# A first token tile projected without its norm factor, and re-split later on GpSimd: the opening stage of a hybrid encoder block

## The chip, the cores and the metric

The kernel runs on one core of a Trainium2 chip. The time is device microseconds of one execution of the whole program, taken as the median of the runs. Names used below: PE is TensorE (matrix products, and transposes as products with an identity), DVE is VectorE, ACT is ScalarE, POOL is GpSimd, SP is SyncE, which issues most of the DMAs. "PEclk" is the share of TensorE's full clock that the chip granted.

## The reference

One layer of an encoder on 512 tokens of width 2048, all in float32. What matters here is its very beginning:

```
def rmsnorm(x, w):
    x32 = x.astype(F32)
    y = x32 * lax.rsqrt(jnp.mean(x32 * x32, axis=-1, keepdims=True) + EPS) * w.astype(F32)
...
        h = rmsnorm(x, norm_w[layer])
        proj = h @ w_in[layer]
        (a_q, a_f, a_i, a_g, c_q, c_kv, k_idx_raw, w_idx_raw, b_g, m_a, m_b) = jnp.split(
            proj, SPLIT_POINTS, axis=-1)
```

Each token has one norm factor, 1 / sqrt(mean of its squares + EPS). Behind the projection come a gated linear recurrence (branch A), an attention over selected keys (branch B), gates, an output projection, the residual and a last norm. Since the factor is one number for each token, h @ W is the factor times (x * w) @ W, token by token.

## The kernel before, in words

Every float32 product is made of three: each operand is split into a high half, which is the value rounded to the product's own number format, and a low half, the rest; high x high, low x high and high x low are added in PSUM. A split costs one copy (the high half, on ScalarE) and one subtraction (the low half, on VectorE or GpSimd).

The program is a list of jobs that are written out one after the other; each engine runs its instructions in the order in which they are written. There is no scheduler: the order in the text is the order on the engine, and engines wait for each other by semaphores alone. The first job that works is `start`. It normalises x, transposes it to [channel, token], splits it into the tiles `xh` and `xl`, which all later projections read, and meanwhile projects 272 columns (256 of `a_i` for the first pair of heads, 16 of the index weights) so that TensorE has something to do. It does so by 4 token tiles t of 128 tokens, and for each of these by 4 groups g of 4 x 128 channels:

- `turn(t, g)` (L313): four transposes of x on TensorE into a PSUM bank `pt`.
- `square(t, i)` (L299): ScalarE squares half a tile of x and sums it along the row. `rstd(t)` (L302, L303) adds the two sums on VectorE and takes the root on ScalarE; `on_diag(t)` (L306, L307) takes the reciprocal and writes it on the diagonal of a 128x128 matrix; `spread()` (L339, L341) multiplies this with ones on TensorE, which gives the factor as a row over tokens in all partitions, and copies it out of PSUM.
- For t = 0: `weigh` (L318) multiplies the transposed x with the norm weight, and the `scaled` at L399 multiplies the result with the factor once this is known. For t = 1 to 3, `follow(t)` does both in one instruction for each 128 channels (L350).
- `high(t, g)` (L322, ScalarE) writes the high half into `xh`, `low(t, g)` (L326) the low half into `xl`: on VectorE, and for t > 0 and odd g on GpSimd.
- The weights come in four blocks `fr` of 512 rows x 272 columns. `w_high(i)` (L330, ScalarE) and `w_low(i)` (L333) split them into `fh` and `fl`; the last block's low half is made on GpSimd.
- `project(t)` makes the products of tile t, 4 groups of 12 (L81: for each group four high x high, four low x high, four with the low weights), and in the middle, ahead of group 2, writes out `follow(t + 1)`. At the end the result is copied to `hv` (L384, ScalarE) and `widx` (L385, VectorE).

Ahead of the last two groups of tile 3 `prep(0)` splits the first weights of the next job (L72 on ScalarE, L73 on VectorE); that job (`kx`, L76 to L78) starts on TensorE as soon as the last product of `project(3)` is through. Of the other names: `ident` is an identity matrix, `wc` holds the norm weight by channel, `st` the sums and factors, `rrow` the factor's row. The loads are issued by SyncE (L272 for x, L277 for the weights); a load may be issued only when the one eight places ahead has landed.

Of the kernel before, what the change touches and what calls it, by code (L numbers as in the profile page):

```python
# [26 lines left out]
F32 = mybir.dt.float32  # L27
# [7 lines left out]
T, D = 512, 2048  # L35
# [15 lines left out]
def hybrid_block(ctx, tc, x, norm_w, w_in, lb_table, gnorm_a, q_norm_w, kv_norm_w, w_uq,  # L51
# [198 lines left out]
    def start():  # L250
# [8 lines left out]
        ys = [p0.tile([128, 4, 128], F32, name=f"y{g}") for g in range(4)]  # L259
        diag = p0.tile([128, 128], F32, name="diag")  # L260
        sq = p0.tile([128, HF], mybir.dt.bfloat16, name="sq")
# [8 lines left out]
        def load_x(t):  # L270
            for i in range(2):
                SP.dma_start(xs[t][i], x2[t * 128:(t + 1) * 128, i * HF:(i + 1) * HF])  # L272

        def load_w(i):
# [16 lines left out]
        for _ in range(4):  # L291
            PE.matmul(warm[:, 0:128], ones, ones, start=True, stop=True)
# [3 lines left out]
        V.tensor_copy(wc, pw[:, 0:16])  # L296

# [19 lines left out]
        def weigh(pt, g):  # L317
            V.tensor_tensor(ys[g], pt.rearrange("p (j t) -> p j t", j=4),  # L318
                            wc[:, g * 4:g * 4 + 4, None].to_broadcast([128, 4, 128]), op=OP.mult)

        def high(t, g):
            A.activation(xh[g][:, :, t * 128:t * 128 + 128], ys[g], AF.Copy)  # L322

        def low(t, g):
            o = slice(t * 128, t * 128 + 128)
            (G if t and g % 2 else V).tensor_tensor(xl[g][:, :, o], ys[g], xh[g][:, :, o].bitcast(F32),  # L326
                                                    op=OP.subtract)

        def w_high(i):
            A.activation(wh[i], raw[i], AF.Copy)  # L330
# [6 lines left out]
        def spread():  # L337
            pr = mmp.tile([128, T], F32, name="acc")
            PE.matmul(pr[:, 0:128], ones, diag, start=True, stop=True)  # L339
            r = p0.tile([128, 128], F32, name="rrow", bufs=2)  # L340
            V.tensor_copy(r, pr[:, 0:128])  # L341
            return r

        def follow(t):
            pts = [turn(t, g) for g in range(4)]
            r = spread()

            def scaled(g):
                for j in range(4):
                    V.scalar_tensor_tensor(ys[g][:, j, :], pts[g][:, j * 128:j * 128 + 128],  # L350
                                           wc[:, g * 4 + j:g * 4 + j + 1], r, op0=OP.mult, op1=OP.mult)
                high(t, g)

            scaled(0)
            scaled(1)
            low(t, 0)
            if t < 3:
                square(t + 1, 0)
            scaled(2)
            low(t, 1)  # L360
            if t < 3:
                square(t + 1, 1)
            scaled(3)
            if t < 3:
                rstd(t + 1)
            low(t, 2)
            if t < 3:
                on_diag(t + 1)
            low(t, 3)

        def project(t):
            o = slice(t * 128, t * 128 + 128)
            acc = mmp.tile([128, T], F32, name="acc")
            for g in range(4):
                if g == 2:
                    if t < 3:
                        follow(t + 1)
                    else:
                        prep(0)
                for n, (xp, wp) in enumerate(((xh, wh), (xl, wh), (xh, wl))):  # L380
                    for k in range(4):
                        mm(acc[:, 0:272], xp[g][:, k, o], wp[g][:, k, :], g + n + k == 0,
                           g + n + k == 8)
            A.activation(v[:, t, :], acc[:, 0:256], AF.Copy)  # L384
            V.tensor_copy(widx[:, t, :], acc[:, 256:272])  # L385

        pts = [turn(0, g) for g in range(4)]
        weigh(pts[0], 0)
        weigh(pts[1], 1)
        square(0, 0)  # L390
        square(0, 1)
        rstd(0)
        on_diag(0)
        w_high(0)
        weigh(pts[2], 2)
        r = spread()

        def scaled(g):
            V.tensor_tensor(ys[g], ys[g], r[:, None, :].to_broadcast([128, 4, 128]), op=OP.mult)  # L399
            high(0, g)  # L400

        scaled(0)
        scaled(1)
        w_low(0, V)
        w_high(1)
        low(0, 0)
        weigh(pts[3], 3)
        square(1, 0)
        scaled(2)
        low(0, 1)  # L410
        scaled(3)
        w_low(1, V)
        w_high(2)
        w_low(2, V)
        square(1, 1)
        low(0, 2)
        rstd(1)
        low(0, 3)
        on_diag(1)
        w_high(3)  # L420
        w_low(3, G)
# [7 lines left out]
        for t in range(4):  # L429
            project(t)  # L430
# [1129 lines left out]
```

## Time and profile before

| | |
|---|---|
| median of 3 runs | 1364.27 us (1363.95 to 1364.37) |
| the profiled execution | 1364.41 us, of which the span of the instructions is 1362.6 us |
| TensorE busy | 1346.5 us, 99% of the span |
| VectorE, ScalarE, GpSimd busy | 1064.7, 655.6 and 42.0 us |
| granted clock, mean | 0.996 |
| first product of the next job (`kx`, L76) | 47.10 us after the start |

The page groups an execution by engines and lines; the views drawn from the trace behind it show the same by order of time (the timeline), by who waited for whom (the waits), as the chain of work that ended last, and as busy times in stretches of one's choice. All times are microseconds from the start of the span. In the rows, `out<-in` names the tiles that an instruction writes and reads, a number ahead of "x" at the end tells how many instructions a row merges, and the bracket tells how long the engine was idle before and what released it. A "q" behind an engine's name means its sequencer, which waits, configures or issues loads while the engine itself does nothing.

### The profile page before, as it was taken

The page shows a single profiled execution, that of the slowest core. Times are in us where ns is not written, and L with a number is a line of the kernel's source. Part 1 is how long each engine was busy: PE and PEld are TensorE (multiplying, and loading weights), DVE is VectorE, ACT ScalarE, POOL GpSimd, SP SyncE. Part 2 cuts the span into 40 slices and gives each one's busy share as a digit, 9 for nine tenths or more (in the row PEclk, how much of TensorE's full clock was granted, in tenths as well). Part 3 has the DMA queues.
Part 4 walks back from the last instruction along what each step waited for, and adds up shares of the span by engine and source line. Part 5 has one row for each costly group of instructions (what it writes and reads, how often), then busy time and mean ns, then how long its engine had stood idle before and what let it go on. Part 6 is the DMA issues. An engine that isn't in the chain of part 4 may idle for free.

```text
span 1362.6 us, 26723 instructions
## 1 busy us (share of the span) xinstructions
PE 1346.5 (99%) x10940; PEld 1251.6 (92%) x10940; DVE 1064.7 (78%) x1742; ACT 655.6 (48%) x1049; POOL 42.0 (3%) x57
## 2 busy tenths in 40 slices
PE   8999999999999999999999999999999999999997
PEld 7888999999999999999999798888888888899996
DVE  7896889998898888886777888775556658899856
ACT  5555445445554445445655353546434334454435
POOL 2100000000000000000000000020101100000000
PEclk8999999999999999999999999999999999999999
DMA  6334355544453445545334433435856556643554
GB/s 207 94 108 140 96 154 157 159 148 136 131 148 110 135 151 146 147 142 166 102 104 125 139 86 118 130 112 184 269 166 202 190 184 211 209 155 111 172 202 165
DMA packets 144732, 204.77 MB, mean 150 GB/s; under 512 B 10537, under 2 KB 85986, under 8 KB 144482
## 3 DMA queue, kind: packets, MB, share of 16 engines
q1 hardware_dynamic: 144322, 202.75, 47.8%
q8 instruction: 85, 1.39, 0.4%
q14 instruction: 37, 0.30, 0.1%
q10 hardware_dynamic: 288, 0.33, 0.1%
HBM read 167.89 MB, written 35.15 MB: 149 GB/s over the span
## 4 chain that ended last, share of the span: by engine, by line
PE 94%; DVE 3%; ACT 1%; issue 0%; DMA 0%; SPq 0%; DVEq 0%; ACTq 0%
PE pp L76 15%; PE pp L78 15%; PE pp L77 15%; PE acc L76 13%; PE acc L78 13%; PE acc L77 13%; PE hl L81 2%; PE acc L81 1%; PE ho L81 1%; PE sc L76 1%; PE sc L77 1%; PE sc L78 1%; PE pt L313 0%; PE hp L81 0%; PE po L78 0%
## 5 line engine op out<-in xcount | busy, mean ns | idle before, releaser
L150 ACT ACTIVATE bh<-wr 128x768 fp32r<-128x768 f32 x128 | 108.2, 845 | 218.4 <-issue 108.3
L152 ACT ACTIVATE wh<-sv 128x512 fp32r<-128x512 f32 x256 | 151.9, 623 | 85.6 <-DVE sv L145 66.1
L73 DVE TENSOR_TENSOR wl<-wr,wh 128x1024 fp32r<-128x1024 f32 (+1 forms) x104 | 125.6, 1208 | 60.9 <-ACT wh L72 60.6
L78 PE MATMUL pp<-sh,wl 128*128 128x256 f32 x624 | 172.8, 277 | 0.0
L76 PE MATMUL pp<-sh,wh 128*128 128x256 f32 x624 | 172.7, 277 | 0.0
L77 PE MATMUL pp<-sl,wh 128*128 128x256 f32 x624 | 172.7, 277 | 0.0
L154 DVE TENSOR_TENSOR wl<-sv,wh 128x1024 fp32r<-128x1024 f32 x128 | 156.5, 1222 | 7.2 <-ACT wh L152 1.1
L153 DVE TENSOR_TENSOR bl<-wr,bh 128x768 fp32r<-128x768 f32 x128 | 122.3, 955 | 50.7 <-ACT bh L150 50.2
L72 ACT ACTIVATE wh<-wr 128x1024 fp32r<-128x1024 f32 (+1 forms) x104 | 108.1, 1041 | 108.6 <-PE acc L77 57.5
L76 PE MATMUL acc<-xh,wh 128*128 128x512 f32 x304 | 121.4, 399 | 0.0
L78 PE MATMUL acc<-xh,wl 128*128 128x512 f32 x304 | 118.6, 390 | 0.0
L77 PE MATMUL acc<-xl,wh 128*128 128x512 f32 x304 | 118.5, 390 | 0.0
L77 PEld LDWEIGHTS pp<-sl,wh 128*128 128x128 f32 x624 | 117.3, 188 | 0.0
L78 PEld LDWEIGHTS pp<-sh,wl 128*128 128x128 f32 x624 | 117.3, 188 | 0.0
L76 PEld LDWEIGHTS pp<-sh,wh 128*128 128x128 f32 x624 | 117.3, 188 | 0.0
L76 PE MATMUL pp<-xh,bh 128*128 128x256 f32 x416 | 114.9, 276 | 0.0
L78 PE MATMUL pp<-xh,bl 128*128 128x256 f32 x416 | 114.9, 276 | 0.0
L77 PE MATMUL pp<-xl,bh 128*128 128x256 f32 x416 | 114.9, 276 | 0.0
L76 PE MATMUL acc<-yh,wh 128*128 128x512 f32 x256 | 100.2, 391 | 0.0
L78 PE MATMUL acc<-yh,wl 128*128 128x512 f32 x256 | 99.8, 390 | 0.0
L77 PE MATMUL acc<-yl,wh 128*128 128x512 f32 x256 | 99.7, 390 | 0.0
L145 DVE TENSOR_TENSOR sv<-wr 128x512 f32<-128x512 f32 x128 | 87.8, 686 | 9.9 <-DMA wr<-in_w_in_dram 7.5
(390 smaller groups left out, 3640.0 us busy)
## 6 DMA issues: line engine op xcount, KB each, us to landing
wr<-in_w_in_dram SPq DMA_DIRECT2D x136, 512.0 KB, 3.8
wr<-in_w_out_dram SPq DMA_DIRECT2D x32, 512.0 KB, 3.6
mg<-gate_d SPq DMA_DIRECT2D x48, 256.0 KB, 4.7
gate_d<-c SPq DMA_DIRECT2D x44, 256.0 KB, 5.3
wr<-in_w_in_dram SPq DMA_DIRECT2D x36, 256.0 KB, 3.0
wr<-in_w_pa_dram SPq DMA_DIRECT2D x16, 512.0 KB, 6.4
wr<-in_w_pb_dram SPq DMA_DIRECT2D x16, 512.0 KB, 4.3
x<-in_x_dram SPq DMA_DIRECT2D x8, 512.0 KB, 4.8
```

The source lines that it names most:

```text
L72: A.activation(hi, src, AF.Copy)
L73: V.tensor_tensor(lo, src, hi.bitcast(F32), op=OP.subtract)
L76: PE.matmul(ps, lh, rh, start=first, stop=False, skip_group_check=True)
L77: PE.matmul(ps, lh, rl, start=False, stop=False, skip_group_check=True)
L78: PE.matmul(ps, ll, rh, start=False, stop=last, skip_group_check=True)
L81: PE.matmul(ps, l, r, start=first, stop=last, skip_group_check=True)
L145: V.tensor_tensor(sv[:, 0:2, :], b[:, 1:3, :], b[:, 0:1, :].to_broadcast([128, 2, 256]), op=OP.add)
L150: A.activation(bh, b[:, 1:4, :], AF.Copy)
L152: A.activation(vh[:, i:i + 2, :], sv[:, i:i + 2, :], AF.Copy)
L153: V.tensor_tensor(bl, b[:, 1:4, :], bh.bitcast(F32), op=OP.subtract)
L154: V.tensor_tensor(vl, sv, vh.bitcast(F32), op=OP.subtract)
```

## The change

The first token tile is projected without its norm factor. Its split is made of x times the norm weight alone, in new tiles `us`, and the products start before any sum of squares is there. When the products of tile 0 are through, `finish()` reads them out with the factor: ScalarE scales `hv`, VectorE scales `widx`. Since later jobs read tile 0 of `xh` and `xl` with the factor in it, these are made anew: the factor's row of tile 0 (`r0`, spread through `diag0`) is multiplied onto `us` by GpSimd (`factor(g)`), and the new halves are copied by ScalarE and subtracted by GpSimd (`renew(g)`), two groups in `project(1)` and two in `project(2)`. The last products of tile 0 (those with the low weights of block 3) are moved behind the first group of tile 1. The high halves of the weight blocks 0 and 3 go from ScalarE to GpSimd. The second half of tile 0's squares moves into `follow(1)`. The low halves of tile 0 are all on VectorE, those of odd groups elsewhere on GpSimd as before. The loads are put in the order of use: the first 512 columns of x, weight block 0, the other three quarters of x's first tile, weight block 1, and on as before. Two further warm-up products stand ahead of the first transposes.

```diff
         SP.dma_start(nw, norm_w.rearrange("o (k d) -> (o k) d", d=128))
-        load_x(0)
+        load_part(0)
         load_w(0)
+        for j in range(1, 4):
+            load_part(j)
         load_w(1)
...
         def w_high(i):
-            A.activation(wh[i], raw[i], AF.Copy)
+            if i % 3 == 0:
+                G.tensor_copy(wh[i], raw[i])
+            else:
+                A.activation(wh[i], raw[i], AF.Copy)
...
+        def factor(g):
+            G.tensor_tensor(us[g], us[g], r0[:, None, :].to_broadcast([128, 4, 128]), op=OP.mult)
+
+        def renew(g):
+            high(0, g, us[g])
+            low(0, g, us[g], G)
...
+        def project(t, before=None):
             acc = mmp.tile([128, T], F32, name="acc")
             for g in range(4):
                 if g == 2:
                     if t < 3:
-                        follow(t + 1)
+                        pts = [turn(t + 1, j) for j in range(4)]
+                        r = spread(row())
+                        if t == 1:
+                            spread(r0, diag0)
+                        follow(t + 1, pts, r)
+                        factor(2 * t - 2)
+                        factor(2 * t - 1)
                     else:
                         prep(0)
...
+                three(t, acc, g, range(3))
+                if g == 0 and before:
+                    before()
             A.activation(v[:, t, :], acc[:, 0:256], AF.Copy)
             V.tensor_copy(widx[:, t, :], acc[:, 256:272])
+            if t < 3:
+                renew(2 * t - 2)
+                renew(2 * t - 1)
...
+        def finish():
+            three(0, acc, 3, (2,))
+            rstd(0)
+            V.reciprocal(st[:, 0, 3:4], st[:, 0, 2:3])
+            A.activation(v[:, 0, :], acc[:, 0:256], AF.Copy, scale=st[:, 0, 3:4])
+            V.tensor_scalar(widx[:, 0, :], acc[:, 256:272], st[:, 0, 3:4], None, op0=OP.mult)
+            V.tensor_scalar(diag0, ident, st[:, 0, 3:4], None, op0=OP.mult)
...
-        for t in range(4):
-            project(t)
+        for t in range(1, 4):
+            project(t, finish if t == 1 else None)
```

The order of the instructions is changed on all engines. On GpSimd, before, from its second instruction with data to the end of the stage (`fl` and `fr`, `fh` are the weights' low halves, raw blocks and high halves; `xl` and `xh` those of x; the number behind a name tells tiles apart, 90 and 93 standing for groups 2 and 3 together; ISA stands for the two entries that configure GpSimd):

```order
L293 MEMSET rows 128x128
L333 ISA
L333 TENSOR_TENSOR fl_135<-fr_150,fh_131 128x1088
L326 TENSOR_TENSOR xl_95<-y_119,xh_92 128x4x128
L326 TENSOR_TENSOR xl_93<-y_121,xh_90 128x4x128
```

And now the same place:

```order
L305 MEMSET rows 128x128
L343 CAST fh_134<-fr_144 128x1088
L343 CAST fh_137<-fr_158 128x1088
L348 ISA
L348 TENSOR_TENSOR fl_141<-fr_158,fh_137 128x1088
L339 TENSOR_TENSOR xl_95<-y_119,xh_92 128x4x128
L339 TENSOR_TENSOR xl_93<-y_121,xh_90 128x4x128
L339 TENSOR_TENSOR xl_95<-y_119,xh_92 128x4x128
L339 TENSOR_TENSOR xl_93<-y_121,xh_90 128x4x128
L368 TENSOR_TENSOR u_122<-u_122,r_126 128x512
L368 TENSOR_TENSOR u_123<-u_123,r_126 128x512
```

Two casts of weight blocks have come ahead of the configuring entries and of the first subtraction, and the multiplications with the factor follow the two low halves of tile 2. On ScalarE, before, from the read-out of tile 1 to the next job's first weights:

```order
L384 ACTIVATE hv<-acc 128x256
L322 ACTIVATE xh_91<-y_118 128x4x128
L322 ACTIVATE xh_92<-y_119 128x4x128
L322 ACTIVATE xh_90<-y_120 128x4x128
L322 ACTIVATE xh_90<-y_121 128x4x128
L384 ACTIVATE hv<-acc 128x256
L72 ACTIVATE wh<-wr 128x512 x3
```

And now:

```order
L420 ACTIVATE hv<-acc 128x256
L335 ACTIVATE xh_91<-u_122 128x4x128
L335 ACTIVATE xh_92<-u_123 128x4x128
L335 ACTIVATE xh_91<-y_118 128x4x128
L335 ACTIVATE xh_92<-y_119 128x4x128
L335 ACTIVATE xh_90<-y_120 128x4x128
L335 ACTIVATE xh_90<-y_121 128x4x128
L420 ACTIVATE hv<-acc 128x256
L335 ACTIVATE xh_90<-u_124 128x4x128
L335 ACTIVATE xh_90<-u_125 128x4x128
L72 ACTIVATE wh<-wr 128x512 x3
```

The copies of the renewed groups 0 and 1 (`u_122`, `u_123`) stand ahead of tile 3's own, those of groups 2 and 3 ahead of the next job's weights. On TensorE, now, from the last products of tile 0 to the second spread:

```order
L81 MATMUL acc<-fh_137,xl_93 128x272 x4
L81 MATMUL acc<-fh_134,xh_91 128x272 x4
L81 MATMUL acc<-fh_134,xl_94 128x272 x4
L81 MATMUL acc<-fl_138,xh_91 128x272 x4
L81 MATMUL acc<-fl_141,xh_90 128x272 x4
L81 MATMUL acc<-fh_135,xh_92 128x272 x4
L81 MATMUL acc<-fh_135,xl_95 128x272 x4
L81 MATMUL acc<-fl_139,xh_92 128x272 x4
L326 MATMUL pt<-ident,x_114 128x128 x8
L326 MATMUL pt<-ident,x_115 128x128 x8
L354 MATMUL acc<-diag,ones_r 128x128
L354 MATMUL acc<-diag_128,ones_r 128x128
```

And before, the same work:

```order
L81 MATMUL acc<-fh_131,xl_93 128x272 x4
L81 MATMUL acc<-fl_135,xh_90 128x272 x4
L81 MATMUL acc<-fh_128,xh_91 128x272 x4
L81 MATMUL acc<-fh_128,xl_94 128x272 x4
L81 MATMUL acc<-fl_132,xh_91 128x272 x4
L81 MATMUL acc<-fh_129,xh_92 128x272 x4
L81 MATMUL acc<-fh_129,xl_95 128x272 x4
L81 MATMUL acc<-fl_133,xh_92 128x272 x4
L313 MATMUL pt<-ident,x_114 128x128 x8
L313 MATMUL pt<-ident,x_115 128x128 x8
L339 MATMUL acc<-diag,ones_r 128x128
```

The product with the last low weights (`fl_135`, now `fl_141`) has moved behind the first group of tile 1, and a second spread has come in.

More of the change, by code (lines that the diff above doesn't have):

```diff
@@ L259, in start @@
         ys = [p0.tile([128, 4, 128], F32, name=f"y{g}") for g in range(4)]
+        us = [p0.tile([128, 4, 128], F32, name=f"u{g}") for g in range(4)]
+        r0 = p0.tile([128, 128], F32, name="r0")
         diag = p0.tile([128, 128], F32, name="diag")
+        diag0 = p0.tile([128, 128], F32, name="diag0")
         sq = p0.tile([128, HF], mybir.dt.bfloat16, name="sq")
@@ L290, in start, with heat @@
         warm = bank("warm")
-        for _ in range(4):
-            PE.matmul(warm[:, 0:128], ones, ones, start=True, stop=True)
+        def heat(n):
+            for _ in range(n):
+                PE.matmul(warm[:, 0:128], ones, ones, start=True, stop=True)
+        heat(4)
         G.memset(rows, 0.0)
@@ L335, in start, with spread, row @@
         v = hg[0, "v"] = R.v0.tile([128, 4, 256], F32, name="hv")
-        def spread():
+        def spread(r, diag=diag):
             pr = mmp.tile([128, T], F32, name="acc")
             PE.matmul(pr[:, 0:128], ones, diag, start=True, stop=True)
-            r = p0.tile([128, 128], F32, name="rrow", bufs=2)
             V.tensor_copy(r, pr[:, 0:128])
             return r
[L344 to L357, printed above, removed]
+        def row():
+            return p0.tile([128, 128], F32, name="rrow", bufs=2)
@@ new lines, in scaled, with follow @@
+        def scaled(t, g, pt, r):
+            for j in range(4):
+                V.scalar_tensor_tensor(ys[g][:, j, :], pt[:, j * 128:j * 128 + 128],
+                                       wc[:, g * 4 + j:g * 4 + j + 1], r, op0=OP.mult, op1=OP.mult)
+            high(t, g, ys[g])
+        def factor(g):
[3 more added lines that the diff above has]
+            low(0, g, us[g], G)
+        def follow(t, pts, r):
+            nxt = t < 3
+            scaled(t, 0, pts[0], r)
+            scaled(t, 1, pts[1], r)
+            low(t, 0, ys[0], V)
+            if t == 1:
+                square(0, 1)
+            if nxt:
@@ L371, in project, with three @@
-        def project(t):
+            low(t, 3, ys[3], G)
+        def three(t, acc, g, which):
             o = slice(t * 128, t * 128 + 128)
+            for n in which:
+                xp, wp = ((xh, wh), (xl, wh), (xh, wl))[n]
+                for k in range(4):
+                    mm(acc[:, 0:272], xp[g][:, k, o], wp[g][:, k, :], g + n + k == 0,
+                       g + n + k == 8)
+        def project(t, before=None):
             acc = mmp.tile([128, T], F32, name="acc")
@@ L389, in start @@
         weigh(pts[1], 1)
+        low(0, 0, us[0], V)
+        high(0, 1, us[1])
         square(0, 0)
[L391 to L394, printed above, removed]
-        weigh(pts[2], 2)
[L396 to L404, printed above, removed]
+        three(0, acc, 0, (0,))
+        pts.append(turn(0, 2))
+        w_low(0, V)
@@ L405, in start @@
+        three(0, acc, 0, (1,))
+        pts.append(turn(0, 3))
+        three(0, acc, 0, (2,))
+        weigh(pts[2], 2)
+        high(0, 2, us[2])
         w_high(1)
-        low(0, 0)
+        low(0, 1, us[1], V)
         weigh(pts[3], 3)
+        w_low(1, V)
+        high(0, 3, us[3])
+        three(0, acc, 1, (0, 1))
+        low(0, 2, us[2], V)
         square(1, 0)
[L409 to L412, printed above, removed]
         w_high(2)
+        low(0, 3, us[3], V)
@@ L414, in start @@
+        square(1, 1)
         w_low(2, V)
-        square(1, 1)
-        low(0, 2)
         rstd(1)
-        low(0, 3)
+        w_high(3)
         on_diag(1)
-        w_high(3)
         w_low(3, G)
+        pts = [turn(1, g) for g in range(4)]
+        three(0, acc, 1, (2,))
+        three(0, acc, 2, (0, 1, 2))
+        r = spread(row())
+        three(0, acc, 3, (0, 1))
+        follow(1, pts, r)
+        def finish():
[5 more added lines that the diff above has]
+            V.tensor_scalar(diag0, ident, st[:, 0, 3:4], None, op0=OP.mult)
```

41 lines of the change are left out of this document (22 added, 19 removed).

## Prediction

> **What bounds the kernel now.** I read the page first, for the bound of the whole.
>
> ```profile
> span 1362.6 us, 26723 instructions
> ...
> PE 1346.5 (99%) x10940; PEld 1251.6 (92%) x10940; DVE 1064.7 (78%) x1742; ACT 655.6 (48%) x1049; POOL 42.0 (3%) x57
> ```
>
> TensorE is idle for 1362.6 - 1346.5 = 16.1 us in all. Whatever delays it in the opening stage is added to the end, since no later gap can take it up. So the change is worth what it does to the moment at which the job behind the stage starts. The chain of waits, next, shows what ends last inside the stage.
>
> ```profile
> 13.72 4.90 PE acc L81 x20
> ...
> 20.88 0.38 PE acc L339 x2
> 21.27 6.25 PE acc L81 x48
> ...
> 29.26 0.45 PE acc L339 x2
> ...
> 38.17 9.06 PE acc L81 x72
> ```
>
> From 13.7 us on the chain is TensorE's own work but for short pieces around the factor's spread (L339, at 20.9 and 29.3): 13.7 is where a lead can be won, and from there any new wait on TensorE is a loss. The busy time by stretches, cut where the granted clock changes, shows the other weakness (columns: stretch, its length, then busy us of PE, PEld, DVE, ACT, POOL, the clock, DMA share, GB/s).
>
> ```profile
> 9.31:12.72 3.41, 1.51 (x8) 0.85 (x7) 3.34 (x7) 2.34 (x4) 0.00 (x0) 1.00 1.02 383
> 12.72:16.13 3.41, 2.43 (x11) 2.42 (x11) 3.41 (x7) 2.50 (x5) 0.00 (x0) 0.50 1.15 337
> 16.13:19.55 3.42, 3.42 (x17) 3.42 (x17) 2.93 (x3) 2.64 (x4) 0.00 (x0) 0.50 1.01 392
> ```
>
> After a stretch in which TensorE worked 1.51 of 3.41 us, the clock stood at half for 3.41 + 3.42 = 6.83 us: up to 3.4 us of work lost.
>
> **The change, part by part.** The timeline gives the places that now matter (columns: start, us, engine, line, operation, what ended the idle time).
>
> ```profile
> 1.03 0.29 POOL L265 CAST ones_r<-rows 128x128 fp32r<-128x128 f32 x1
> 1.17 1.28 ACT L289 ACT_TABLE_LOAD   x1 [1.17 <-PEq L1544]
> L333 POOLq MODIFY_POOL_CONFIG  x2: 11/11/11, 1.5 to 1.6; - x2
> SPq L424 <- DMA fr<-in_w_in_dram: 0.9, 1, 0.9
> 16.86 0.25 SPq L425 DMA_DIRECT2D rows<-in_kidx_norm_w_dram  x1
> 19.96 1.10 ACT L330 ACTIVATE fh<-fr 128x1088 fp32r<-128x1088 f32 x1
> 21.14 2.56 POOL L333 TENSOR_TENSOR fl<-fr,fh 128x1088 fp32r<-128x1088 f32 x1 [19.55 <-ACT fh L330]
> ...
> 23.75 0.77 PE L81 MATMUL acc<-fl,xh 128*128 128x272 f32 x4
> 24.36 0.66 PE L81 MATMUL acc<-fh,xh 128*128 128x272 f32 x4
> 25.86 0.66 PE L81 MATMUL acc<-fh,xh 128*128 128x272 f32 x4
> 29.45 0.75 PE L81 MATMUL acc<-fh,xh 128*128 128x272 f32 x4
> ```
>
> *First loads and tile 0 without its factor.* The loads move the same bytes at the 337 to 392 GB/s of the stretches above, so the last weight block lands as before: SyncE's small load L424 waited 0.9 us on its large part, and the one of 16.86 behind it on its small one. The first products can start earlier, since they no longer wait for the sum over the whole row. In the forecast this buys nothing, since TensorE then stands at the last weight block, as follows; the rivals price the case in which it counts. The two extra warm-up products run while x is on its way: nothing.
>
> *The last weight block on GpSimd.* Its high half was a ScalarE instruction of 1.10 us. As a GpSimd cast it is bounded below by that, and above by the 128-element cast's 0.29 taken 1088/128 times, 2.5 (GpSimd's two-input 2.56 on the same shape is no less); I take the middle, 1.8. It ends at 16.9 + 1.8 = 18.7.
>
> *GpSimd's configuration.* Its two MODIFY_POOL_CONFIG entries ran at 1.5 us, and the first subtraction followed at 21.14, with 19.55 us between that hid whatever they set off. Now two casts that wait for landed weights stand ahead of them in GpSimd's queue, so they are reached near 18.7, with the subtraction right behind. What they cost no run shows. The ends are 1.28 (ScalarE's table load, the one code-like load with a duration) and 19.6 (all that was hidden). Neither row is near; I take 7.7, midway between the logarithmic middle (5.0) and the plain one (10.4). [...]
>
> So the subtraction runs from 18.7 + 7.7 = 26.4 to 29.0. TensorE takes its product ahead of tile 1's second group: at 29.0 instead of 23.75. The products of tile 1's first group (24.36 to 25.86, 1.5 us) are by then done, so tile 1's second group starts at 29.5 against 25.86: +3.6. GpSimd's next piece, that group's low half, ends 1.3 later (rows below), 0.3 after it is wanted, and the second spread (r0), right behind the first, takes about half of the 0.45 in the chain, 0.25: at the row of 29.45, +4.2. Before this TensorE has stood for some 4.6 us, longer than the sparse stretch above. I add the cold clock at half of its 3.4: +1.7, bounds 0 and 3.4. Sum at 29.45: **+5.9**.
>
> *The renewal.* Four multiplications and four subtractions go to GpSimd, four copies to ScalarE, and they stand in those queues ahead of work that TensorE waits for.
>
> ```profile
> 36.16 1.32 POOL L326 TENSOR_TENSOR xl<-y,xh 128x512 fp32r<-128x512 f32 x1 [1.90 <-ACT xh L322]
> 40.62 0.68 DVE L326 TENSOR_TENSOR xl<-y,xh 128x512 fp32r<-128x512 f32 x1
> 40.73 0.63 ACT L322 ACTIVATE xh<-y 128x512 fp32r<-128x512 f32 x1 [0.40 <-DVE y L350]
> 41.03 0.67 PE L81 MATMUL acc<-fh,xh 128*128 128x272 f32 x4
> 41.54 0.66 PE L81 MATMUL acc<-fh,xl 128*128 128x272 f32 x4
> 44.11 1.30 POOL L326 TENSOR_TENSOR xl<-y,xh 128x512 fp32r<-128x512 f32 x1 [1.38 <-ACT xh L322]
> 44.20 1.14 ACT L72 ACTIVATE wh<-wr 128x512 fp32r<-128x512 f32 x2
> 47.10 0.48 PE L76 MATMUL acc<-xh,wh 128*128 128x512 f32 x1
> 47.65 0.39 PE L78 MATMUL acc<-xh,wl 128*128 128x512 f32 x1
> ```
>
> In the times of before: GpSimd is done at 37.5 with tile 2's last low half, then multiplies groups 0 and 1 (1.3 each, to 40.1). ScalarE copies the second to 40.7, and only then splits tile 3's first group, to 41.3; its product starts at 41.3 instead of 41.03. VectorE's low half of it (0.68) wants to run from 41.3, and GpSimd subtracts there until 42.7. That such pieces exclude one another these rows show:
>
> ```profile
> 20.43 0.29 DVE L307 TENSOR_SCALAR diag<-ident,st 128x128 f32<-128x128 f32 x1
> 27.73 1.34 POOL L326 TENSOR_TENSOR xl<-y,xh 128x512 fp32r<-128x512 f32 x1 [1.91 <-ACT xh L322]
> 28.07 1.08 DVE L307 TENSOR_SCALAR diag<-ident,st 128x128 f32<-128x128 f32 x1
> 49.70 0.69 DVE L73 TENSOR_TENSOR wl<-wr,wh 128x512 fp32r<-128x512 f32 x1 [3.14 <-ACT wh L72]
> ```
>
> The same diag took 0.29 alone and 1.08 inside GpSimd's 27.73 to 29.07. So tile 3's second product starts 0.5 to 1.7 after its 41.54, by who comes first; GpSimd's own low half for tile 3, behind the two renewals, makes the lower end 1.0. I take **+1.3**.
>
> At the end, tile 3's last low half ends at 45.4. Groups 2 and 3 are multiplied to 48.0, ScalarE copies the last to 48.6, and only then makes the next job's high half (half of the 1.14 row, 0.6): the product of 47.10 starts at 49.2, +2.1. Of that 0.1 was already waited for above: +2.0. Its low half (0.69) then meets GpSimd's last two subtractions (48.0 to 50.6), so the product of 47.65, now due at 49.8, gets it between 49.9 and 51.2: +0.7. Together **+2.7**.
>
> *The read-out.* This stands in front of the second spread:
>
> ```profile
> 24.36 1.04 ACT L299 ACTIVATE sq<-x 128x1024 bf16<-128x1024 f32 x1
> ...
> 27.17 0.16 DVE L302 TENSOR_TENSOR st<-st 128x1 f32<-128x1 f32 x1 [0.70 <-ACT sq L299]
> 27.56 0.28 ACT L303 ACTIVATE st<-st,cols 128x1 f32<-128x1 f32 x1
> 27.75 0.36 ACT L384 ACTIVATE hv<-acc 128x256 f32<-128x256 f32 x1
> 27.87 0.16 DVE L306 RECIPROCAL st<-st 128x1 f32<-128x1 f32 x1
> 29.07 0.16 DVE L385 COPY widx<-acc 128x16 f32<-128x16 f32 x1
> ```
>
> The extra square, with the read of its sum, delays tile 2's factor by 1.1. Sum, root, reciprocal, scaled read-out, scaled index weights and the second diagonal come to 0.16 + 0.28 + 0.16 + 0.36 + 0.16 + 0.29 and some 0.1 between engines = 1.5. In the forecast all of it is done while TensorE stands at the weight block; without that cover it costs up to 1.1 + 1.5 + 0.25.
>
> **Sum:** 5.9 + 1.3 + 2.7 = +9.9 on the profiled execution's 1364.41 (span 1362.6 and 1.8 around it); the median of the runs, 1364.27, lies 0.14 lower: **1374.2 us**.
>
> **The rivals.**
>
> *A. The configuration costs next to nothing.* For it: the two entries show 11 ns each. Then the subtraction follows the cast from 18.7 to 21.3 and the bound is tile 1's factor. Its sum on VectorE waits out the cast, to 18.7 or, when a weight subtraction goes first, 19.3; sum, root, reciprocal and diagonal take 0.9 behind that. So its spread comes at 20.1, or at 22.1 if GpSimd's subtraction gets in ahead of the diagonal (21.3 + 0.8); before at 20.9. From there the row of 29.45 was 8.6 later; with 1.1 + 1.5 it is 11.2 later: +1.9 to +3.9. With 1.3 + 2.7: +5.9 to +7.9, middle 6.9: **1371.2**.
>
> *B. The load is longer than 10.5*, up to the 19.6 that were hidden: +2.8 to +11.9 on the forecast, from **1377.0**.
>
> *C. The lead is kept (not slower).* TensorE's first products come early enough to fill the stretch up to 12.7, and the half clock behind it goes. With GpSimd out of VectorE's way tile 1's spread comes at 18.8 (20.1 less the wait for the cast, 1.3), 2.1 early. The place where it decides is the product of the last low weight block: only if GpSimd delivers by the end of tile 1's first group (24.36 + 1.5 - 2.1 = 23.8), configuration included, does TensorE not stand there. The lead pays for most of the read-out chain (18.8 + 11.2 = 30.0 against 29.45, +0.5), the renewal costs 2.0 at the end without exclusion: +2.5, **1366.8**, within 0.2%. Against it: the 1.08 row shows the exclusion.
>
> *D. The lead is kept and the renewal is hidden too*, as if GpSimd's pieces fitted between ScalarE's: the half clock's 3.4 us are won, **1360.9**. Against it: in the order ScalarE's copies wait for GpSimd directly ahead of the next job's split.
>
> **How the numbers follow.** Forecast 0.60, A 0.22, B 0.05, C 0.10, D 0.03. I count 0.2% (2.7 us) as what a measurement of this kernel can tell from no change. Slower: forecast, A and B, 0.87. Same: C, 0.10. Faster: D, 0.03. The range: A's low end is +5.9, and its renewal at its lowest (1.0 + 2.1 instead of 1.3 + 2.7) makes it +5.0; 1368.5 (+4.2) leaves 0.8 for pieces that happen not to meet. The forecast's high end is a load of 10.5 (+2.8) with the clock's full 3.4 (+1.7): 1378.7. Together 1368.5 to 1379.0 hold the forecast and A, 0.82; B, C and D are left out.
>
> **What would show it.** In the new profile: the first subtraction of weights on GpSimd several us after its second cast with nothing shown between; TensorE idle before the low-weight product of tile 0's fourth group, released by GpSimd; a half clock behind it; ScalarE waiting for GpSimd's multiplications, and TensorE for the next job's first high and low halves. Wrong if GpSimd's subtraction follows its cast at once (A), and wholly wrong if the next job's first product starts before 48 us (C, D).

## The result, and the profile of the changed kernel

The changed kernel takes 1376.12 us (median of 6 runs, 1375.52 to 1377.36) against 1364.32 before (1363.95 to 1365.2): 1.0085 times as long, 95% interval 1.0075 to 1.0096, or 11.8 us more. The profiled execution took 1377.36, of which the span is 1375.5, 12.9 more than before's span; it lies 1.2 above the median. The page's head (engines' busy time) shows that TensorE was also busy longer, though it does almost the same products:

```profile
span 1375.5 us, 26744 instructions
...
PE 1351.6 (98%) x10944; PEld 1253.1 (91%) x10944; DVE 1068.6 (78%) x1738; ACT 655.5 (48%) x1051; POOL 55.1 (4%) x67
```

Busy time grew by 5.1 us, with products that take longer at half clock (0.63 each from 56.73 on, 0.39 from 59.96 on), and idle time by 7.8, from 16.1 to 23.9. What TensorE waited for in the whole execution (us in total, times, the longest):

```profile
PE acc L354 <- DVE diag L320: 3.6, 2, 2.8
PE acc L76 <- ACT wh L72: 1.9, 1, 1.9
...
PE acc L354 <- DVE diag L473: 1.1, 1, 1.1
PE acc L78 <- DVE wl L73: 1.1, 1, 1.1
PE acc L81 <- DVE xl L339: 1.1, 1, 1.1
PE ns L81 <- DVE suml L73: 0.8, 1, 0.8
```

The largest is the wait for tile 1's diagonal. The rows of three engines around it, from the timeline, with the configuring entries ahead of them:

```profile
L348 POOLq MODIFY_POOL_CONFIG  x2: 3/3/3, 19.0 to 19.0; - x2
17.42 1.64 POOL L343 CAST fh<-fr 128x1088 fp32r<-128x1088 f32 x1 [9.57 <-DMA fr<-in_w_in_dram]
19.14 2.48 POOL L348 TENSOR_TENSOR fl<-fr,fh 128x1088 fp32r<-128x1088 f32 x1
...
18.02 1.05 DVE L315 TENSOR_TENSOR st<-st 128x1 f32<-128x1 f32 x1
19.43 0.17 DVE L319 RECIPROCAL st<-st 128x1 f32<-128x1 f32 x1 [0.36 <-ACT st L316]
19.63 2.07 DVE L320 TENSOR_SCALAR diag<-ident,st 128x128 f32<-128x128 f32 x1
...
21.75 0.49 PE L354 MATMUL acc<-diag,ones_r 128*128 128x128 f32 x2 [2.82 <-DVE diag L320]
```

The two configuring entries (3 ns each at 19.0) stand between the cast, which ends at 19.06, and the subtraction at 19.14: they cost next to nothing. The sum of two numbers (0.15 before) took 1.05, to the cast's end, and the diagonal (0.29) took 2.07, to the subtraction's end at 21.62. TensorE had its first products at 8.08 (11.97 before), ran out of work at 18.9 and stood 2.82. Below, a lock means just this: a VectorE instruction ends only with the GpSimd instruction that started ahead of it. Not all are caught: the reciprocal at 19.43 took 0.17 inside the same subtraction, 0.15 before.

The second place is the end of the stage:

```profile
44.76 1.82 DVE L339 TENSOR_TENSOR xl<-y,xh 128x512 fp32r<-128x512 f32 x1 [0.56 <-ACT xh L335]
...
46.63 0.78 PE L81 MATMUL acc<-fh,xl 128*128 128x272 f32 x4 [1.08 <-DVE xl L339]
...
50.63 2.52 POOL L368 TENSOR_TENSOR u<-u,r 128x512 f32<-128x512 f32 x2
53.11 2.50 POOL L339 TENSOR_TENSOR xl<-u,xh 128x512 fp32r<-128x512 f32 x2
...
53.19 0.63 ACT L335 ACTIVATE xh<-u 128x512 fp32r<-128x512 f32 x1 [0.60 <-POOL u L368]
53.72 1.13 ACT L72 ACTIVATE wh<-wr 128x512 fp32r<-128x512 f32 x2
...
54.37 2.40 DVE L73 TENSOR_TENSOR wl<-wr,wh 128x512 fp32r<-128x512 f32 x2 [4.58 <-ACT wh L72]
...
54.39 0.49 PE L76 MATMUL acc<-xh,wh 128*128 128x512 f32 x1 [1.86 <-ACT wh L72]
...
56.22 0.71 PE L78 MATMUL acc<-xh,wl 128*128 128x512 f32 x1 [1.10 <-DVE wl L73]
```

ScalarE's copy of the last renewed group waits for GpSimd's multiplication, and the next job's weights stand behind it; then VectorE's low halves (0.69 each alone) lie locked beside GpSimd's subtractions. What followed shows in the stretches that the clock's changes cut out (length, then busy us of PE, PEld, DVE, ACT, POOL, the clock, DMA share, GB/s):

```profile
18.79:22.20 3.41, 0.59 (x5) 0.45 (x4) 2.51 (x3) 0.29 (x1) 2.74 (x2) 1.00 0.71 249
22.20:25.62 3.42, 2.96 (x14) 2.62 (x13) 3.31 (x12) 1.45 (x3) 0.11 (x1) 0.50 0.58 153
...
52.93:56.34 3.41, 0.85 (x3) 0.42 (x4) 1.97 (x2) 1.67 (x3) 2.69 (x3) 1.00 0.00 0
56.34:59.75 3.41, 3.41 (x9) 2.63 (x10) 0.42 (x1) 0.52 (x1) 0.00 (x0) 0.50 0.56 154
```

Each of these two sparse stretches (TensorE busy for 0.59 and 0.85) is followed by one at half clock. The first falls where TensorE waits for others anyway. The second falls on the next job, where TensorE itself sets the pace (0.43 from product to product at 57.15 instead of 0.23 at 60.19). Last, the products L81 of that job's sums (`ns`) stood 0.84 for `suml`, since ScalarE's `wh` ahead of `sumh` came late:

```profile
72.14 1.06 ACT L72 ACTIVATE wh<-wr 128x1024 fp32r<-128x1024 f32 x1 [3.00 <-DMA wr<-in_w_in_dram]
```

Instruction by instruction the delay against before therefore grows so: +3.7 at tile 1's third group (33.14 against 29.45), +5.1 at tile 3's first low half (46.63 against 41.54), +7.3 at the next job's first product (54.39 against 47.10), +8.6 at its first low weights (56.22 against 47.65), +10.3 behind the half clock, +11.4 behind the sums. From there to 800 us it stays near 11.4; small delays behind that, 1.7 in all, bring this one execution's last product to +13.0 and its span to +12.9.

### The profile page after: what moved, and what is told of

Its sections match the earlier page's. It is cut to its first block, busy times and chain, and to the rows that moved or that the text cites. A ratio compares the mean times of both kernels' runs of the same rounds, so it can differ in the third digit from the quotient of the medians.

```text
span 1375.5 us, 26744 instructions
## 1 busy us (share of the span) xinstructions
PE 1351.6 (98%) x10944; PEld 1253.1 (91%) x10944; DVE 1068.6 (78%) x1738; ACT 655.5 (48%) x1051; POOL 55.1 (4%) x67
## 4 chain that ended last, share of the span: by engine, by line
PE 89%; DVE 4%; ACT 2%; DMA 2%; POOL 1%; issue 1%; SPq 0%; ACTq 0%; POOLq 0%; DVEq 0%
PE pp L76 15%; PE pp L77 15%; PE pp L78 15%; PE acc L76 12%; PE acc L77 12%; PE acc L78 12%; PE hl L81 2%; DMA fr<-in_w_in_dram 1%; PE ho L81 1%; DVE wl L73 1%; PE sc L76 1%; PE sc L77 1%; PE sc L78 1%; POOL xl L339 1%; DMA wr<-in_w_in_dram 1%
```

## The experiments

The theory: locks between GpSimd and VectorE and the order in ScalarE's queue make the waits, and waits make half clocks. The rivals stand with each run. All medians are of 4 to 11 runs. The last columns are from each profiled execution, a single one that lies up to 1.3 us off its kernel's median: the start of the next job's first product, and the time of the load on which its sums depend, from its issue to its landing by the DMA records.

| run | median us | ratio to before (95%) | next job | load |
|---|---|---|---|---|
| before | 1364.3 to 1364.9 | | 47.10 | 3.6 |
| changed kernel | 1376.12 | 1.0085 (1.0075 to 1.0096) | 54.39 | 4.9 |
| e1_cast_scalar | 1374.04 | 1.0066 (1.0054 to 1.0079) | 51.09 | 4.7 |
| e2_no_renewal | 1369.74 | 1.0040 (1.0027 to 1.0054) | 50.84 | 4.7 |
| e3_weights_first | 1374.46 | 1.0070 (1.0057 to 1.0083) | 51.71 | 5.1 |
| e4_loads_only | 1368.09 | 1.0026 (1.0017 to 1.0035) | 49.05 | 4.6 |
| e5_factor_early | 1371.62 | 1.0050 (1.0037 to 1.0062) | 49.19 | 4.9 |
| e6_renew_spread | 1366.74 | 1.0016 (1.0007 to 1.0025) | 47.84 | 4.9 |
| e7_factor_first | 1366.68 | 1.0015 (1.0006 to 1.0024) | 46.87 | 4.9 |
| e8_warm_wait | 1378.77 | 1.0101 (1.0087 to 1.0115) | 56.13 | |
| e9_warm_short | 1382.32 | 1.0129 (1.0115 to 1.0142) | 64.79 | |
| e10_before_warm | 1367.38 | 1.0019 (1.0010 to 1.0028) | 49.08 | 4.9 |
| e11_both | 1366.27 | 1.0012 (1.0003 to 1.0021) | 46.41 | 4.8 |
| e12_fewer_passes | 1364.47 | 0.9996 (0.9986 to 1.0005) | 46.56 | 3.7 |

**e1_cast_scalar: the lock at tile 1's diagonal.**

```diff
-            if i % 3 == 0:
+            if i == 0:
                 G.tensor_copy(wh[i], raw[i])
```

> The changed kernel with the cast of weight block 3 back on ScalarE, behind tile 1's root; block 0's stays on GpSimd. Theory (GpSimd's cast and subtraction held VectorE's sum for 0.90 and its diagonal for 1.78 us): the sum takes 0.15 again, the diagonal stands ahead of GpSimd's subtraction and takes 0.29, and tile 1's factor is spread near 19.2 instead of 21.75; tile 1's third group starts 2 to 2.6 earlier than its 33.14, and the median falls by 2 to 4, to 1372-1374 (the upper end of the gain if the half clock at 22 goes too). Rival 1 (the diagonal was late for another reason, its wait for the root or the loads): the spread stays near 21.7 and the time within 0.7 of 1376.1. Rival 2 (the spread is earlier but the lead is lost at the read-out chain): spread near 19.2, third group still near 33, no gain.

In its timeline the sum and the diagonal run alone again, the spread comes 3.6 earlier than 21.75, and the read-out's two waits stay:

```profile
17.11 0.15 DVE L315 TENSOR_TENSOR st<-st 128x1 f32<-128x1 f32 x1
17.83 0.28 DVE L320 TENSOR_SCALAR diag<-ident,st 128x128 f32<-128x128 f32 x1
...
18.17 0.49 PE L354 MATMUL acc<-diag,ones_r 128*128 128x128 f32 x2
27.68 0.49 PE L354 MATMUL acc<-diag,ones_r 128*128 128x128 f32 x2 [0.84 <-DVE diag L320]
29.31 0.76 PE L354 MATMUL acc<-diag,ones_r 128*128 128x128 f32 x2 [1.14 <-DVE diag L473]
29.72 1.25 PE L81 MATMUL acc<-fh,xh 128*128 128x272 f32 x4
```

The lock is shown: tile 1's third group is 3.4 earlier. A half clock now follows the read-out's waits (0.50 from 29.38 to 32.79; the four products of 1.25 took 0.75 in the changed kernel), but the next job is still 3.3 earlier and the last product too. The medians differ by only 2.1, the near end of the expectation: the changed kernel's profiled execution is the slowest of its six (1375.52 to 1377.36; here 1372.84 to 1374.13).

**e2_no_renewal: the price of the renewal.**

```diff
-                        factor(2 * t - 2)
-                        factor(2 * t - 1)
...
-            if t < 3:
-                renew(2 * t - 2)
-                renew(2 * t - 1)
```

> The changed kernel without the renewal: the four multiplications of tile 0 by its factor's row on GpSimd, the four copies and the four subtractions are left out, so tile 0 of xh and xl stays without the factor for all later jobs; the read-out with the factor and the second spread stay. Theory (the renewal costs 1.4 at tile 3's low half, 1.9 and 1.1 at the next job's first weights, 1.7 by the half clock that these set off and 1.1 at the sums behind it: 7.2 to 7.7): the next job's first product comes 3.5 to 3.7 later than before's 47.10, at 50.7, no half clock behind it, median 1368.0 to 1369.0. Rival 1 (the renewal only delays pieces that have room, and the half clock and late loads follow from the late start alone): 1372 or more. Rival 2 (the renewal costs only the 2.7 + 1.3 of the forecast): 1372.1.

1369.74: 6.4 of the 11.8 us are the renewal's. The next job started at 50.84, behind the last product of tile 3 without a wait, and at full clock (0.23 from product to product). The other 5.4 are the start (+3.7) and what the later runs explain; the expected 7.2 to 7.7 was 1 too high, because the sums wait 0.8 in this run as well.

**e3_weights_first: ScalarE's order alone.**

```diff
-                        prep(0)
+                        prep(-1)
+                        renew(2)
+                        renew(3)
+                        prep(0)
```

(and `renew` at the end of `project` for groups 0 and 1 only.)

> The changed kernel with the copies and subtractions of the renewed groups 2 and 3 written behind the splits of the next job's first two weight blocks instead of ahead of them; the multiplications stay where they are. Theory (the queue order on ScalarE is what delays the next job): wh is made from 49.6 on, the next job's first product follows the last of tile 3 near 52.3 without a wait, no half clock, median 1370 to 1372. Rival (the locks between GpSimd and VectorE decide): wl waits out the multiplications that now run beside it (50.6 to 53.2), TensorE waits 1 to 2 us at its first product, the half clock stays, and the median is 1373.5 to 1375.

The next job started right behind the last of tile 3, at the full clock (0.23 from product to product), as the theory said: the order is what delayed it. The median, 1374.46, fell by 1.7 only, as the rival said, but not where it said so. VectorE's low halves now lay beside the multiplications, as in this row,

```profile
49.58 2.79 DVE L73 TENSOR_TENSOR wl<-wr,wh 128x512 fp32r<-128x512 f32 x2 [0.35 <-ACT wh L72]
```

which held no product up. But the second of the loads behind them was issued at 52.39, when these low halves ended, 1.7 behind the first (0.6 in all other runs), and the sums behind the job waited 2.2 instead of 0.8, for a load that was issued late and then took 5.1. So the locks did cost time, by way of a load. Neither expectation is met as a whole.

**e4_loads_only: the load order by itself.** The kernel before with `load_part` and `heat(2)`, and nothing else.

> The kernel before with the new order of the loads and the two further warm-up products, nothing else. Theory (the loads move the same bytes and the last weight block lands as before; the sum over tile 0's row then sets the start): within 0.7 of 1364.3. Rival (the first weight block ahead of the rest of x delays tile 0's squares, factor and products): first product over 1 us later than before's 11.97, and 1365.3 or more.

3.5 slower: the rival. ScalarE's second half of the squares waits for x (9.16 against 7.36), and everything behind the factor comes 2.0 later, the next job too:

```profile
9.16 1.06 ACT L309 ACTIVATE sq<-x 128x1024 bf16<-128x1024 f32 x1 [0.78 <-DMA x<-in_x_dram]
```

The other 1.5 are the sums (0.8) and small delays later on. Whether the order pays in the changed kernel, whose first products don't need all of x, no run tests alone.

**e5_factor_early: the read-out chain.** On top of e1:

```diff
         high(0, 1, us[1])
-        square(0, 0)
+        square(0, 1)
...
+        PE.matmul(pr[:, 128:256], ones, diag0, start=True, stop=True)
+        PE.matmul(pr[:, 0:128], ones, diag, start=True, stop=True)
```

(with `square(0, 0)` behind `high(0, 0)`, `rstd(0)` behind `low(0, 1)`, reciprocal and `diag0` behind `low(0, 3)`, and none of these in `finish()`.)

> The first experiment's kernel (cast of block 3 on ScalarE), and tile 0's own factor made early: both halves of its squares on ScalarE before 11 us, its sum, root, reciprocal and diagonal in the opening, its row spread next to tile 1's in one PSUM bank; finish() only reads out. Theory (the read-out chain and the extra square cost 1.14 + 0.84 of TensorE's waits there and the half clock at 29.4 behind them): tile 2's factor is spread near 26.6 without a second wait, tile 1's third group starts near 26.8 instead of 29.72, no half clock at 29, the renewal costs its 7 as before, median 1368 to 1370. Rival (the chain is paced elsewhere, by the second half of the squares or VectorE): third group after 28.5, median over 1371.5.

Both waits of the read-out and the half clock at 29 are gone:

```profile
27.67 0.39 PE L354 MATMUL acc<-diag,ones_r 128*128 128x128 f32 x2
27.81 0.75 PE L81 MATMUL acc<-fh,xh 128*128 128x272 f32 x4
```

The spread of tile 2, expected at 26.6, comes no earlier than in e1 (27.68), since tile 1's is 0.8 later; but no second spread follows it, and tile 1's third group starts 1.9 earlier. 2.4 won on e1. The renewal still costs what it did (waits of 1.9 and 1.1 at the next job's first weights, half clock at 50.85).

**e6_renew_spread and e7_factor_first: the renewal in the gaps, and tile 1's factor first.** From the change of e6 (`renew` is split into its copies and its subtractions, here `rest`; `factor(0)` stands ahead of `follow(1)`):

```diff
             low(t, 1, ys[1], G)
+            (None, factor, rest, rest)[t]((None, 1, 0, 3)[t])
...
             low(t, 3, ys[3], G)
+            if t == 1:
+                factor(2)
+                factor(3)
+            if t == 2:
+                rest(1)
+                rest(2)
```

On top of this, e7 puts `square(1, 1)` ahead of `w_high(2)`, `rstd(1)` and `on_diag(1)` ahead of `w_low(2, V)`, and the spread ahead of that block's product.

> The same with the renewal's eight GpSimd pieces put singly or in pairs where VectorE works on products with the factor's row: the four multiplications during tile 1, one subtraction between tile 2's two low halves, two behind them, one between tile 3's, none ahead of the next job; the copies where ScalarE waits. Nothing is left out. Theory (the renewal's price is where its pieces meet VectorE's short subtractions and the next job's splits, not the work as such): TensorE waits neither at tile 3 nor at the next job's first weights, no half clock at 56, the next job's first product near 45, and the median is 1361.5 to 1363.5, under the kernel before. Rival 1 (13 us of GpSimd work take VectorE's time wherever they stand): waits of 2 or more in tiles 2 and 3, 1365 to 1368. Rival 2 (an earlier start is lost to the half clock): half clock before 30, 1364 to 1366.

> The same, with tile 1's second half of the squares ahead of weight block 2's high half on ScalarE, its sum, reciprocal and diagonal ahead of that block's low half on VectorE, and the spread ahead of that low half's product on TensorE. Theory (tile 1's factor sets the pace of all that follows): the spread comes 0.5 to 1 earlier than in the run before it, and so does the next job; median 1361 to 1363. Rival (weight block 2 is then late and TensorE waits for it instead): no earlier, or later by up to 1.

Both came to 1366.7. The renewal's part of the theory held: no wait at tile 3 and none at the next job. The size did not, and the rest of the lead went at a new lock, at the renewal's own first multiplication. In e6, GpSimd subtracts weight block 3 until 21.68 and multiplies group 0 only then, beside tile 1's first low half (0.68 alone):

```profile
19.18 2.50 POOL L348 TENSOR_TENSOR fl<-fr,fh 128x1088 fp32r<-128x1088 f32 x1 [11.48 <-ACT fh L345]
21.64 1.28 POOL L368 TENSOR_TENSOR u<-u,r 128x512 f32<-128x512 f32 x1
...
21.80 1.67 DVE L339 TENSOR_TENSOR xl<-y,xh 128x512 fp32r<-128x512 f32 x1
...
23.53 1.12 PE L81 MATMUL acc<-fh,xl 128*128 128x272 f32 x4 [1.19 <-DVE xl L339]
```

e7 has the same wait, and its spread came later, not earlier (19.30 against 18.67): the rival, since TensorE waited 0.8 for blocks 1 and 2. Its profiled execution has no half clock behind 13 us, e6's has one from 23.73 (four products take 1.12 there, 0.77 in e7). That half clock seems to cost time: of e6's eleven runs, the four with a mean clock of 0.998 or more took 1365.5 to 1366.7, the other seven 1365.8 to 1369.4, with a median of 1367.6.

**e8_warm_wait, e9_warm_short: filling the wait.** e8 has 18 products of ones behind the last transpose; e9 has 9 in that transpose's own bank:

```diff
         V.tensor_copy(cols[:, 0:25], pt[:, :25])
+        for _ in range(9):
+            PE.matmul(pt[:, 128:256], ones, ones, start=True, stop=True)
```

> The changed kernel with 18 products of ones behind the last transpose of the opening stage, in the 2.1 us in which TensorE waits for the next job's weights. Theory (the half clock from 56.3 to 59.8 is set off by that wait): it goes, and the median falls by 1.0 to 1.9, to 1374.2-1375.1. Rival (the clock follows something else, or the 1.1 of wait that remains at the low half is enough): half clock in the same place, time within 0.5 of 1376.1 or above.

> The changed kernel with 9 products of ones (18 passes in the records) behind the last transpose of the opening stage, written into the free half of that transpose's bank so that no later bank changes place; the run before this one had twice as many passes (4.2 us) and another bank. Theory (the half clock from 56.3 to 59.8 is set off by TensorE's wait of 1.9 + 1.1 for the next job's first weights): the next job runs at the full clock and the median falls by 1.0 to 1.7, to 1374.4-1375.1. Rival (the 1.1 of wait that is left is enough for the half clock, or the clock follows something else): half clock in the same place, within 0.6 of 1376.1.

In e8 the next job did run at the full clock (0.23 from product to product), and behind it the profile was 1.2 ahead of the changed kernel's although the filler, 36 passes in 4.2 us, held it up by 1.7; so with the wait filled that half clock did not come. Its time, 2.7 above the changed kernel's, does not bear this out and does not refute it: near 767 us TensorE stood 1.8 with no releaser shown, and lost some 3.5 there with the half clock that followed (products of 0.63 instead of 0.40). e9 misses its aim: its products had to wait for VectorE's copy out of the same bank,

```profile
60.93 1.43 PE L488 MATMUL pt<-ones_r 128*128 128x128 f32 x5 [8.30 <-DVE cols L486]
```

and three stretches of half clock followed, 56.5 to 66.8. It adds only that a longer wait (8.3 instead of 1.9) was followed by a longer half clock (10.3 instead of 3.4).

**e10_before_warm: before's half clock taken away.**

```diff
+            for _ in range(heat):
+                PE.matmul(pr[:, 128:256], ones, ones, start=True, stop=True)
...
-        r = spread()
+        r = spread(7)
```

> The kernel before with 7 products of ones behind the first spread, in the 1.8 us in which TensorE waits for the first split. Theory (before's half clock from 12.7 to 19.6 is off the path, since tile 1's factor, on its diagonal at 20.4, ends later than TensorE's products): the half clock goes or moves, the next job still starts at 46.6 to 47.2, and the median is within 0.7 of 1364.5. Rival (the half clock's 3.4 us of work are on the path, as rival D of the prediction had it): 1361 to 1362.5.

2.6 slower than before, an outcome of neither: the row's copy (L343) had to wait for the filler in its bank, 2.1.

```profile
12.17 0.29 DVE L343 COPY rrow<-acc 128x128 f32<-128x128 f32 x1 [2.08 <-PE acc L341]
```

But the run bears on its question. The clock stood at full from 10.7 on (1.00 in the stretches up to 17.53; before's was 0.50 from 12.72 on), and the 1.9 lost at the copy were still 2.0 at tile 1's third group and at the next job (49.08): a full clock from there on won back nothing. The 71 repeated runs of the kernel before, which this copy does not disturb, say the same: the 20 with a mean clock of 0.999, which leaves at most 4.1 us of recorded half clock in the whole execution, have a median span of 1362.85, the 15 with 0.996, like the profiled one, 1362.5. Before's half clock was off the path, and rival D's 3.4 was not there to be won.

**e11_both and e12_fewer_passes: the last lock, and a load.** On top of e7, e11 moves `w_low(3, G)` behind tile 1's first GpSimd piece, its product behind tile 2's transposes, and two quarters of x ahead of the first weight block; the renewal's pieces are placed anew, one of its low halves on VectorE. e12 then takes out warm-up products:

```diff
-        heat(4)
+        heat(1)
...
-        heat(2)
```

> The best of the runs so far (factor of both tiles early, renewal spread out), further: the first two quarters of x are loaded ahead of weight block 0; weight block 3's low half on GpSimd stands behind tile 1's first GpSimd low half instead of ahead of it, and its product with tile 0 behind tile 2's transposes; one renewed low half goes to VectorE behind tile 3's last. Theory (in that run VectorE's first low half of tile 1 waited 1.0 for GpSimd's subtraction of block 3, and all that follows kept this delay): the spreads of tiles 1 and 2 are 8.5 apart instead of 9.6, the next job starts at 45.2 to 46.0, and the median is 1364 to 1366, at or just under the kernel before, since the sums behind the next job still wait about 1 for a load. Rival (the delay comes back at another lock): the next job at 46.5 or later, 1366 to 1367.5.

> The kernel of the run before this (e11_both) without five of its six warm-up products, 20 TensorE instructions fewer (a pass and a weight load each, two of both for a product); nothing else. In all traces so far an instruction fetch of 16 KB falls near TensorE's 675th instruction, and in all changed kernels, which have 8 or more such instructions more ahead of the next job than the kernel before, it runs inside the load (issued near 57 there) for which the sums behind the next job wait; that load then takes 4.6 to 5.0 instead of 3.6. Theory (the fetch is what makes the sums wait 0.6 to 1.1): it now falls over 3 us behind the issue of that load, the load takes under 4 us, TensorE's wait at the sums goes, and the median falls by 0.7 to 1.3, to 1365.0-1365.6. Rival (the fetch does not move with the count, or the load is slow for another reason): wait and time as before, 1366.3 within 0.5; later if the missing warm-up costs clock.

In e11 the lock at the low half is gone and another took its place, as its rival had it: a sum of two numbers waited out the moved subtraction.

```profile
23.95 2.53 POOL L349 TENSOR_TENSOR fl<-fr,fh 128x1088 fp32r<-128x1088 f32 x1
...
25.33 1.17 DVE L316 TENSOR_TENSOR st<-st 128x1 f32<-128x1 f32 x1 [0.70 <-ACT sq L313]
```

The next job started at 46.41, 0.7 ahead of before, yet behind the sums the profile was 1.1 late. e12 bears on that. Over the first 2.9 us of the load, the transfers by kind (packets, MB, share of 16 engines; `instruction` is a fetch of 16 KB of instructions, more on it at the end) are, in e11,

```profile
q1 hardware_dynamic: 444, 0.45, 56.3%
q8 instruction: 1, 0.02, 2.7%
```

and in e12

```profile
q1 hardware_dynamic: 467, 0.48, 61.1%
```

With 20 TensorE instructions fewer, the instruction fetch no longer lies in it, and ScalarE gets the block 3.8 after its issue at 57.19 (61.93 for an issue at 57.08 in e11):

```profile
60.95 1.06 ACT L72 ACTIVATE wh<-wr 128x1024 fp32r<-128x1024 f32 x1 [2.34 <-DMA wr<-in_w_in_dram]
```

The median fell by 1.8, to 1364.47: no measurable difference from the kernel before. Not all of this is the load's: of the 1.5 between the two profiled executions 0.9 had come by the sums, the rest beyond 700 us, and was not followed up. TensorE still waits 0.6 at the sums, since the load, not TensorE, is now last there: it was issued 10.6 behind the next job's first product, against 9.8 in before. So the lead of 0.5 at the next job is taken up at this place. No version tried beats the kernel before.

## Why the prediction came out as it did

The time (1374.2 forecast, 1376.1 measured, within 1368.5 to 1379.0) and the sign were right; the mechanism that the forecast put first was not.

- **The step that failed: "I take 7.7" for GpSimd's configuration, and with it the +5.9 at the row of 29.45.** The configuration cost 0.08 at most (cast's end 19.06, subtraction 19.14), which is the prediction's own sign that its mechanism was wrong. The 7.7 was an estimate between two bounds, and no run shows such a cost behind these entries. TensorE never waited for the last low weights. In its place stood rival A, chance 0.22, at its worst end: the diagonal caught behind GpSimd's subtraction, spread at 21.75 (22.1 named), third group +3.7 (+3.9 named). e1 shows the lock to be the cause.
- **The read-out**, counted as hidden, lay open once the configuration did not cover it, again as A had it: 0.74 and 1.14. e5 removes both.
- **The renewal, +1.3 and +2.7**: measured 1.4 at tile 3 (5.1 - 3.7) and 3.5 at the next job (8.6 - 5.1). Mechanism and places were right; the lock at the low weights was worth 1.3 and not 0.7. e2 prices all that follows from it at 6.4.
- **The cold clock, +1.7**: there was one near the place, and it cost nothing that shows, since tile 1 waits for VectorE and ScalarE there. One that was not in the sum cost 1.7, behind the waits at the next job.
- **The sums, +1.1**, were not seen: a load behind the stage, with nothing to spare in before (e12, 0.5 earlier at the next job, waits 0.6 there).
- **The early start "buys nothing"**: no run takes the load order out of the changed kernel, so what it was worth there stays open; in the kernel before, the order costs 3.5 (e4).

So 3.7 + 1.4 + 3.5 + 1.7 + 1.1 = 11.4 replaced 5.9 + 1.3 + 2.7 = 9.9. The agreement of the totals is luck: one term was 2.2 too high, and two that it left out come to 2.8. By rival A's own sum, 1371.2 to 1372.2, the time would have been 4 to 5 too low. The late delays of the profiled execution (1.7, between 815 and 1080 us of before's time) were not followed up; whether instruction fetches have a part in them stays open.

## What to carry to other kernels

Ask of every instruction that moves to GpSimd which VectorE instructions will run beside it, the tiny ones on the chain first: a sum of two numbers (1.05 instead of 0.15) waited about as long as a large tile (1.82 instead of 0.69). Some instructions ran there unharmed: in the changed kernel eight products with the factor's row took 2.16 from 42.04 on, with GpSimd at work all the time, and 2.16 from 22.61 on, with GpSimd idle. A lead won at the start of a stage is kept only if nothing else (a factor's chain, a load, a queue order behind the stage) is due at nearly the same time; look for what is hidden by less than the lead. A wait is to be priced with the half clock behind it, but only where TensorE itself sets the pace: here 1.7 at the next job, and nothing that shows at tile 1. A price from a single profiled execution is good to about a microsecond here.

## What the hardware showed that was not expected

**The clock's windows.** In the traces of the kernel before and of the changed kernel the granted clock is recorded from 9.31 and from 11.96 on, and its changes lie multiples of 3.41 us apart (the half clocks inside the stage last 6.83, 3.41 and 3.41). Cut there into stretches of 3.41, the stretches at full clock that half clock followed are the one of 9.31 in before (TensorE busy for 1.51), those of 18.79 and 52.93 in the changed kernel (0.59 and 0.85), and the last at full clock in each, at the end of the program (0.2 and 0.3). All others were followed by full clock; the sparsest of them is that of 29.03 in the changed kernel, with 1.99. Of the stretches at half clock that of 12.72 in before (2.43) was followed by another, those with 3.42 (before, 16.13), 2.96 and 3.41 (changed kernel, 22.20 and 56.34) by full clock. In e1 a stretch with 1.45 (25.96) and in e2 one with 0.81 (19.38) were followed by half clock; one with 1.64 in e10 was not, the next stood at 1.00:

```profile
10.71:14.12 3.41, 1.64 (x14) 1.45 (x13) 1.92 (x4) 0.90 (x2) 0.00 (x0) 1.00 1.09 357
```

**Instruction fetches.** The page of the changed kernel counts them beside its data:

```profile
q1 hardware_dynamic: 144610, 202.75, 47.3%
q8 instruction: 86, 1.41, 0.4%
```

86 fetches of 16 KB for 2 x 10944 TensorE instructions is one in 254. In before the first four begin behind 175, 417, 663 and 909 of these instructions, in the changed kernel behind 175, 425, 661 and 911, and each of the first three takes 0.9 to 1.2 us. The 2.7% of 16 engines above are 1.25 us of engine time; what a fetch does to the transfers beside it the records don't show engine by engine. What they show is the load at the sums. In the changed kernel a fetch began at 69.23, 2.1 behind the load's issue at 67.12, and ScalarE got the block 5.0 behind the issue; in e11 one lay in the load's first 2.9, and it was 4.8. In before the fetch began at 60.02, 3.1 behind the issue at 56.93, and it was 3.7; in e12, with none in the first 2.9, 3.8. Between e11 and e12 lie twenty TensorE instructions. That the fetch is what makes the load late is the author's reading of these four. Whether TensorE itself ever waited for one is not shown.
